# Fixing TensorE's order through the sample step of a two-layer streaming encoder, with gate products in thirds between its steps

## The chip, the cores and the metric

The kernel runs on one core of one Trainium2 chip. The metric is the time of one execution on the device, in microseconds (us), from the first to the last instruction with what lies around them. Three timed runs of the kernel before gave 2090.80, 2094.46 and 2092.82 us; their median is 2092.82 us. The profile was taken in an execution of its own.

The engines are called as in the profile: PE (TensorE, matrix products), DVE (VectorE), ACT (ScalarE), POOL (GpSimd) and SP (SyncE, which here only issues transfers). Each engine works through its own list of instructions in one order, and waits on semaphores for the others.

## What is computed

The reference is one step of an encoder with two layers, over a prompt of 2048 tokens and 8 samples of 16 tokens, 1024 wide, all in float32. Layer 0 is a diagonal complex state-space mixer (S5), layer 1 a gated delta rule mixer with 8 value heads and states of 128 x 128. Each layer normalizes, shifts, scales and gates with values made from a condition vector.

```python
for i in range(DEPTH):
    mod = silu(c) @ w_ada[i] + b_ada[i]
    shift, scale, gate = split(mod, 3)
    h = rms_norm(x, norm_g[i]) * (1 + scale) + shift
    out, state = s5_branch(h, ...) if i == 0 else gdn_branch(h, ...)
    x = x + gate * out
y = rms_norm(x, final_g)
```

The change lies in layer 1. Its branch projects h to queries, keys, values and a gate z, runs a short convolution over q, k and v, and then, chunk by chunk of 128 tokens and for each head, does the delta rule in matrix form: a triangular matrix made from keys, decays and betas is inverted; new values are that inverse times (beta v minus decayed keys times the old state); the output is decayed queries times the old state plus a masked product of queries and keys with the new values; the state is decayed and gets keys times new values. The output is normalized per head, multiplied by silu(z) and projected by `w_out`. The outputs are y, the states after prompt and samples, and the last rows before the convolution.

## The kernel before

Tokens are ordered in 17 tiles of 128: tiles 0 to 15 are the prompt, and tile 16 holds the 8 samples, each with a state of its own that comes from outside. All products of weights with activations are made in three parts (`mm3`, L148): high by high, high by low, low by high, where a number is split into a high part in a narrower format and the rest.

Layer 1 has these stages, in the order of the code:

- Blocks 0 to 15 (`conv_block`): q, k and v of all tokens, with convolution, written to DRAM as `kq_d` and `v_d`. Between them small triangular blocks are solved on DVE (`lane_solve`).
- Blocks 16 to 23: the gate z, in five column ranges `NATT` (widths 512, 512, 384, 384, 384). `gate_cols` (L1793) makes one block and range: 24 products into one PSUM tile, a SiLU on ACT, and a store to `zz_d` from ACT's queue (`store_heads`). Blocks 16 to 20 come first. Blocks 21 to 23 do their two wide ranges before the sample step; the nine narrow ones stay in the list `rest`, and `between` (L1935) makes one of them each time it is called.
- The entry to the sample step, L1903 to L1907: `load_x(0, 16)` loads tile 16 (keys and queries `kq`, row terms `ra` and `rb`, blocks of the inverse `xf`), adds masks on POOL and takes 16 or 8 exponentials on ACT (`decays`); `k_prod` makes keys by keys and queries by keys; `k_turn` and `v_turn` transpose keys and values on PE and scale them on DVE (`kup`, `bv`).
- The sample step (`sample`, L1390), a loop over 8 heads. `first(h)` loads the 8 samples' states of one head (`s0`, 512 KB) and multiplies keys and queries with them (L1407). `second(h)` takes the new values (L1418), copies them on ACT (`svn`, L1420), makes the output part (L1421), spreads the new values over the samples on DVE (`vm`, L1425), multiplies keys with them (L1428), adds into the states on DVE (L1431) and stores these from POOL's queue (L1433). After head 3 chunk 0 is loaded and its `k_prod` made, after head 5 its block inverse is finished (`invert`).
- The prompt loop (L2135), 16 chunks in order. Each carries the state `Sf` forward, in high and low parts `Sh` and `Sl`. The projection of one tile (`project`) is a generator whose pieces are put between the steps of later chunks, by the string of letters at L2184 (p for a piece of the projection, i for one of the next chunk's inverse, v for half of the next chunk's value turn). The sample tile's projection is the first of them; it leaves the products with the low part of the weight to the end (`late_low`, L2078).
- Before the loop, the last weight `w_out` is loaded (`w2_raw`, 8 parts of 512 KB) and split into high parts on ACT (L2114) and low parts on POOL (L2117).

The order of the work on each engine is set by a planner, which runs the program in a model of its own time and picks the earliest work in program order that is ready there. Two things bind it. `tc.issue_after(i)` (in `later`, L142) lets an instruction come only after `i` in the plan. And an `Engine` whose `ordered` is true puts each of its instructions behind the one before, so its list is just the order of the Python program. In the kernel before SP is ordered from L2121, DVE from L2131, and ACT, PE, DVE and POOL from L2140, at chunk 0; DVE and POOL go back to the planner at L2152, SP at L2182. In the sample step nothing is ordered.

The names that the steps below touch: `ssq` (sums of squares per head), `rs` (their reciprocal roots, made by `rsqrt`, L1347, with two ACT functions and small DVE operations on 8 columns), `oo` (outputs of a tile), `poT` (their transposes), `ob`, `ohi`, `olo` (gated, and split in high and low), `epo` (the projection), `psu` (keys by new values), `pvn` and `vn` (new values of a chunk), `epk` and `epv` (transposed keys and values), `fB` and `gB` (rows spread over all partitions), `ezt` (z of a tile). PSUM pools: `pso` with 2 buffers, `psh` with 4, `pse` with 2. The gate's activations of layer 1 (`h1h`, `h1l`) lie in the same memory as later the weight parts and the chunk's tiles.

## Time and profile before

| | kernel before |
|---|---|
| timed runs, median (3) | 2092.82 us |
| the profiled execution | 2091.16 us |
| its span, first to last instruction | 2089.4 us |
| PE busy | 2039.9 us (98%) |
| DVE busy | 1481.2 us (71%) |
| ACT busy | 1007.9 us (48%) |
| POOL busy | 507.5 us (24%) |
| mean granted PE clock | 0.991 |
| DMA | 343.74 MB, mean 165 GB/s |

In a row of a timeline stand start and length in us, engine, line, operation, what it writes and reads, and the count of like instructions merged; in brackets, the idle time of the engine before it and what ended that. L70 is the line of the helper that issues the instructions of ordered engines, so there the names tell more than the line. Rows with SPq or ACTq are issues of transfers. Matmul ends are modelled, so a group's length reaches a little over the start of the next.

### The profile page before, as it was taken

What the parts mean: (1) busy time and instruction counts of PE and PEld (TensorE: products, weight loads), DVE (VectorE), ACT (ScalarE), POOL (GpSimd) and SP (SyncE); (2) the same over time, 40 slices, a digit from 0 to 9 for tenths busy, and PEclk for the clock granted to TensorE, in tenths of its full rate; (3) what the DMA queues carried; (4) which work ended last, traced back from release to release, by engine and by line L of the source; (5) the groups of instructions that cost most, each with busy time, mean ns of one, the idle gap of its engine ahead of it and who ended that gap; (6) DMA issues with size and microseconds to landing.
All of it is one profiled execution on the core that took longest, in us unless ns stands there. A gap on an engine that the chain in (4) does not pass through costs nothing.

```text
span 2089.4 us, 41295 instructions
## 1 busy us (share of the span) xinstructions
PE 2039.9 (98%) x15473; PEld 1824.0 (87%) x15473; DVE 1481.2 (71%) x3401; ACT 1007.9 (48%) x2426; POOL 507.5 (24%) x759
## 2 busy tenths in 40 slices
PE   7999999999999999999999999999999699999998
PEld 5889988888999999999788879899987588888887
DVE  7988668777674455557555669687546888888885
ACT  4534445555454444446655322341224466666663
POOL 1268500000122222221100010110022444444430
PEclk8999999999999999999999999999999999999999
DMA  8798856666563333325665212753455734455532
GB/s 308 275 309 277 272 169 199 192 193 185 166 206 124 103 121 108 130 93 213 185 192 162 76 50 77 183 137 100 138 170 192 228 124 136 149 151 151 151 116 71
DMA packets 314611, 343.74 MB, mean 165 GB/s; under 512 B 88522, under 2 KB 261082, under 8 KB 311596
## 3 DMA queue, kind: packets, MB, share of 16 engines
q1 hardware_dynamic: 183196, 229.90, 35.6%
q10 hardware_dynamic: 125792, 94.38, 13.9%
q0 software_dynamic: 5424, 16.83, 2.2%
q8 instruction: 122, 2.00, 0.4%
q14 instruction: 77, 0.63, 0.1%
HBM read 220.81 MB, written 120.21 MB: 163 GB/s over the span
## 4 chain that ended last, share of the span: by engine, by line
PE 87%; DVE 5%; DMA 4%; ACT 3%; issue 1%; ACTq 0%; SPq 0%; POOL 0%; DVEq 0%
PE epo L70 8%; PE pdz L70 8%; PE pc L151 5%; PE pc L152 5%; PE pc L153 5%; PE po L153 3%; PE po L152 3%; PE pz L153 3%; PE po L151 3%; PE pz L151 3%; PE pz L152 3%; PE py L70 3%; PE pd L151 2%; PE pg L153 2%; PE pg L151 2%; PE pg L152 2%
## 5 line engine op out<-in xcount | busy, mean ns | idle before, releaser
L151 PE MATMUL pc<-h1h,wdh 128*128 128x512 f32 (+1 forms) x600 | 216.7, 361 | 0.8 <-ACT pb L1570 0.8
L152 PE MATMUL pc<-h1l,wdh 128*128 128x384 f32 (+1 forms) x600 | 215.1, 358 | 0.3 <-POOL h1l L1521 0.3
L153 PE MATMUL pc<-h1h,wdl 128*128 128x384 f32 (+1 forms) x600 | 215.1, 359 | 0.0
L1581 DVE SCALAR_TENSOR_TENSOR ac<-pb,convw,ac 128x384 f32<-128x384 f32 (+3 forms) x288 | 163.7, 592 | 3.3
L151 PE MATMUL po<-gh,woh 128*128 128x272 f32 x512 | 147.9, 292 | 1.7 <-ACT woh L137 1.1
L153 PE MATMUL po<-gh,wol 128*128 128x272 f32 x512 | 148.9, 292 | 0.4 <-DVE wol L139 0.4
L152 PE MATMUL po<-gl,woh 128*128 128x272 f32 x512 | 148.3, 291 | 0.1
L70 PE MATMUL pdz<-hhz,wzh 128*128 128x272 f32 x448 | 131.1, 293 | 0.4 <-ACT evz L70 0.4
L152 PE MATMUL pg<-yl,wgh 128*128 128x272 f32 x448 | 130.0, 290 | 0.0
L151 PE MATMUL pg<-yh,wgh 128*128 128x272 f32 x448 | 129.4, 289 | 0.0
L70 PE MATMUL pdz<-hhz,wzl 128*128 128x272 f32 x448 | 129.3, 289 | 0.0
L153 PE MATMUL pg<-yh,wgl 128*128 128x272 f32 x448 | 129.2, 288 | 0.0
L70 PE MATMUL pdz<-hlz,wzh 128*128 128x272 f32 x448 | 128.8, 288 | 0.0
L151 PEld LDWEIGHTS pc<-h1h,wdh 128*128 128x128 f32 x600 | 112.8, 188 | 13.0 <-ACT pb L1570 1.7
L152 PEld LDWEIGHTS pc<-h1l,wdh 128*128 128x128 f32 x600 | 112.8, 188 | 10.5 <-issue 0.8
L153 PEld LDWEIGHTS pc<-h1h,wdl 128*128 128x128 f32 x600 | 112.7, 188 | 10.1 <-issue 0.8
L151 PE MATMUL pd<-hh,wuh 128*128 128x272 f32 x384 | 112.4, 295 | 2.8 <-ACT hh L229 2.8
L70 PE MATMUL epo<-w2h,ohi 128*128 128x512 f32 x272 | 111.7, 411 | 0.0
L153 PE MATMUL pd<-hh,wul 128*128 128x272 f32 x384 | 111.1, 290 | 0.0
L152 PE MATMUL pd<-hl,wuh 128*128 128x272 f32 x384 | 111.1, 290 | 0.0
L1104 POOL TENSOR_TENSOR zt<-zt,sz 128x272 f32<-128x272 f32 x64 | 61.7, 970 | 192.1 <-ACT sz L1103 188.9
L70 PE MATMUL epo<-w2h,olo 128*128 128x512 f32 x272 | 107.1, 394 | 0.0
(651 smaller groups left out, 6329.4 us busy)
## 6 DMA issues: line engine op xcount, KB each, us to landing
wa<-in_w_ada SPq DMA_DIRECT2D x32, 512.0 KB
wdr<-in_w_in SPq DMA_DIRECT2D x24, 512.0 KB
u_d<-ev ACTq DMA_DIRECT2D x64, 136.0 KB
...
```

Source lines behind the costliest of these rows:

```text
L70: i_ = f(*a, **kw)
L151: T.matmul(ps, lhsT=w_hi[k], rhs=x_hi[k], start=(k == 0), stop=False)
L152: T.matmul(ps, lhsT=w_hi[k], rhs=x_lo[k], start=False, stop=False)
L153: i_ = T.matmul(ps, lhsT=w_lo[k], rhs=x_hi[k], start=False, stop=(k == n - 1))
L1104: G.tensor_mul(zt, zt, sz)
L1581: V.scalar_tensor_tensor(o, src(j), convw[:, b, j:j + 1], o, op0=ALU.mult, op1=ALU.add)
```

## The change

It does these things.

- `sample` calls `between` three times for a head: after `svn` has been copied, after `vm` has been made, and at the end of the head.
- `gate_cols` is divided: `gate_products` makes the 24 products in parts and stops after each, and `gate_store` does the SiLU and the store. The nine narrow blocks become a generator `fills` that gives 27 thirds (9, 9 and 6 products); each call of `between` takes one.
- PE is ordered from the wide gate blocks of 21 to 23 to the end of the sample step.
- In the entry, `k_turn` of tile 16 comes after two thirds, `v_turn` after a third one.
- Chunk 0 is loaded after head 2 (in the plan behind the activation of the last stored block), its `k_prod` comes after head 4, and its inverse runs in one piece per call from head 5 on. The gate blocks are no longer held behind chunk 0's exponentials.
- The low part of `w_out` is made in four quarters of 256 columns. Only parts 0 to 2 are split before chunk 0; high parts 3 to 7 come inside chunk 0 behind the new values, their low parts behind the new state.
- In chunk 0 the sample tile's gate comes first, then the new values, the products of the new state (`state_products`, taken out of `new_state`) and the transposes of chunk 1's keys (`k_transposes`, taken out of `k_turn`), then the transposes of the sample tile (`split`) and the first piece of its projection, and only then the rest of the new state.
- The letters of chunk 0 become "v v p p i p i p" in place of "p p p i v v p i p".

```diff
--- before.py
+++ after.py
@@ -1259,13 +1259,17 @@
         else:
             mm3(ps, [p["kh"][:, s, :]], [p["kl"][:, s, :]], [rh], [r])
 
-    def k_turn(p, E=G):
+    def k_transposes(p):
+        pk = pse.tile([P, 4, P], F32, tag="e", name=f"epk{p['t']}")
+        for h in range(4):
+            T.transpose(pk[:, h, :], p["kq"][:, h, :], ident)
+        return pk
+
+    def k_turn(p, E=G, pk=None):
 
         n, t, kq, kh = (p[i] for i in ("n", "t", "kq", "kh"))
         p["kup"] = kup = epar(n).tile([P, 8, P], F32, tag="kup", name=f"kup{t}")
-        pk = pse.tile([P, 4, P], F32, tag="e", name=f"epk{t}")
-        for h in range(4):
-            T.transpose(pk[:, h, :], kq[:, h, :], ident)
+        pk = pk or k_transposes(p)
         V.tensor_mul(kup.rearrange("p (h r) i -> p h r i", r=2), bc(pk, 2, 2),
                      bc(sc["ku"][:, t].rearrange("p (h r) -> p h r", r=2), 3, P))
         if kh is not None:
@@ -1418,11 +1422,13 @@
             T.matmul(p2[:, 0], lhsT=x[:, h, :], rhs=r, start=True, stop=True)
             vn = es.tile([P, P], F32, tag="sr", name=f"svn{h}")
             S.copy(vn, p2[:, 0])
+            between(h, 0)
             T.matmul(p2[:, 1], lhsT=pt_[:, h, :], rhs=vn, start=True, stop=True)
             V.tensor_add(oo[:, h], oo[:, h], p2[:, 1])
             S.activation(p2[:, 1], oo[:, h], AF.Square, accum_out=ssq[:, h:h + 1])
             vm = (eb1 if h % 2 else ea1).tile([P, 8, P], F32, tag="S", name=f"vm{h}")
             V.tensor_mul(vm, bc(vn, 1, 8), bc(seq, 2, P))
+            between(h, 1)
             for hf in range(2):
                 p4 = psh.tile([P, 4, P], F32, tag="h", name=f"sp4{h}_{hf}")
                 T.matmul(p4, lhsT=kup[:, h], rhs=h4(vm, hf), start=True, stop=True)
@@ -1437,7 +1443,7 @@
             nxa = first(h + 1) if h < 7 else None
             second(h, *a)
             a = nxa
-            between(h)
+            between(h, 2)
         return lambda zt: gate(t, oo, ssq, zt)
 
 
@@ -1790,9 +1796,17 @@
                 nc.sync.dma_start(row_d[w_, 0:128, :], ro[:, 0])
                 nc.sync.dma_start(row_d[w_, 128:136, :], ro[0:8, 1])
 
+        def gate_products(b, w, n0, n, pool, tag, parts=(None,)):
+            ps = pool.tile([P, 512], F32, tag=tag, name=f"pz{b}_{n0}")[:, 0:n]
+            for part in parts:
+                mm3(ps, [w[0][:, k] for k in range(KC)], [w[1][:, k] for k in range(KC)], *hcols(n0, n), part)
+                yield ps
+
         def gate_cols(b, w, n0, n, pool, tag):
-            ps = pool.tile([P, 512], F32, tag=tag, name=f"pz{b}_{n0}")[:, 0:n]
-            mm3(ps, [w[0][:, k] for k in range(KC)], [w[1][:, k] for k in range(KC)], *hcols(n0, n))
+            ps, = gate_products(b, w, n0, n, pool, tag)
+            return gate_store(b, n0, n, ps)
+
+        def gate_store(b, n0, n, ps):
             ac = d3.tile([P, 512], F32, tag="ac", name=f"az{b}_{n0}")[:, 0:n]
             silu = S.activation(ac.rearrange("p (c s) -> p c s", s=8), by_token(ps, n), AF.Silu).ins
             store_heads(zz_d, b - 16, n0, n, ac)
@@ -1902,14 +1916,13 @@
             nc.sync.dma_start(g1_d[:, 512 * hf:512 * hf + 512], g9[0:9])
         p16 = load_x(0, 16)
         k_prod(p16)
-        k_turn(p16)
         load_v(p16)
-        list(v_turn(p16))
 
         wz = {21: wnext}
         t_ = pbp.tile([P, 2, KC, P], F32R, tag="pb", name="wd23")
         wz[22] = load_blk(22 * P, dst=(t_[:, 0], t_[:, 1]))
         wz[23] = load_blk(23 * P)
+        T.ordered, T.last = True, None
         for b, w in wz.items():
             for n0, n in NATT[0:2]:
                 gate_cols(b, w, n0, n, pso, "o")
@@ -1928,25 +1941,41 @@
         y64 = {1: eb1.tile([P, 8, 64], F32, name="y641")}
         for z_ in (xf[1], y64[1]):
             G.memset(z_, 0.0)
-        rest = [(b, w, n0, n) for n0, n in NATT[2:] for b, w in wz.items()]
-
-        p0 = {}
-
-        def between(h=8):
-
-            with later([p0["ex"]] if p0 else []):
-                i_ = gate_cols(*rest.pop(0), pso, "o")
-            if h == 3:
-                with later([i_]):
+        p0, silus, inv = {}, [], []
+
+        def fills():
+            for n0, n in NATT[2:]:
+                for b, w in wz.items():
+                    for ps in gate_products(b, w, n0, n, pso, "o", (range(3), range(3, 6), range(6, KC))):
+                        yield
+                    silus.append(gate_store(b, n0, n, ps))
+
+        fill = fills()
+
+        def between(h, step):
+
+            next(fill, 0)
+            if step == 2 and h == 2:
+                with later(silus[-1:]):
                     p0.update(load_x(1, 0))
-                    k_prod(p0)
-            if h == 5:
-                list(invert(p0))
-            return i_
-
+            if step == 2 and h == 4:
+                k_prod(p0)
+            if step == 2 and h == 5:
+                inv.append(invert(p0))
+            for i in inv:
+                next(i, 0)
+
+        for _ in range(2):
+            next(fill)
+        k_turn(p16)
+        next(fill)
+        list(v_turn(p16))
         sample_gate = sample(p16, between)
-        while rest:
-            last_silu = between()
+        for _ in fill:
+            pass
+        list(inv[0])
+        last_silu = silus[-1]
+        T.ordered = False
     if upto == "D":
         return dict(kq_d=kq_d, v_d=v_d, zz_d=zz_d, row_d=row_d, x1n_d=x1n_d, nd_d=nd_d, xd_d=xd_d, yd_d=yd_d)
 
@@ -2008,14 +2037,20 @@
                 S.copy(vn, p2)
                 p["vn"].append(vn)
 
-        def new_state(p):
-            t, kup = p["t"], p["kup"]
+        def state_products(p):
+            ps = []
+            for hf in range(2):
+                ps.append(psh.tile([P, 4, P], F32, tag="h", name=f"psu{p['t']}_{hf}"))
+                for i in range(4):
+                    T.matmul(ps[hf][:, i], lhsT=p["kup"][:, 4 * hf + i, :], rhs=p["vn"][hf][:, i], start=True, stop=True)
+            return ps
+
+        def new_state(p, ps):
+            t = p["t"]
             nh = ea1.tile([P, 8, P], F32R, tag="S", name=f"Sh{t}")
             nl = eb1.tile([P, 8, P], F32R, tag="S", name=f"Sl{t}")
             for hf in range(2):
-                p3 = psh.tile([P, 4, P], F32, tag="h", name=f"psu{t}_{hf}")
-                for i in range(4):
-                    T.matmul(p3[:, i], lhsT=kup[:, 4 * hf + i, :], rhs=p["vn"][hf][:, i], start=True, stop=True)
+                p3 = ps[hf]
                 if t == 0:
                     V.tensor_copy(h4(Sf, hf), p3)
                 else:
@@ -2110,11 +2145,15 @@
             for k in ks:
                 SY.dma_start(w2_raw[k], I["w_out1"][k * P:(k + 1) * P])
 
-        def split_w2(k):
+        def high_w2(k):
             S.copy(w2_hi[k], w2_raw[k])
+
+        def low_w2(k):
             if k:
                 w2_lo[k] = e1.tile([P, D], F32R, tag=f"w2r{k - 1}", name=f"w2l{k}")
-            nc.gpsimd.tensor_sub(w2_lo[k], w2_raw[k], w2_hi[k].bitcast(F32))
+            for q in range(4):
+                c = slice(256 * q, 256 * q + 256)
+                G.tensor_sub(w2_lo[k][:, c], w2_raw[k][:, c], w2_hi[k][:, c].bitcast(F32))
 
         y64[0] = eb.tile([P, 8, 64], F32, name="y640")
         G.memset(y64[0], 0.0)
@@ -2125,8 +2164,9 @@
         zt = load_z(16)
         gates = project_rows(16)
         pp = {0: p0, 1: load_x(2, 1, True)}
-        for k in range(KC):
-            split_w2(k)
+        for k in range(3):
+            high_w2(k)
+            low_w2(k)
         k_turn(p0)
         V.ordered = True
         list(v_turn(p0))
@@ -2139,13 +2179,18 @@
                 for e in (S, T, V, G):
                     e.ordered = True
                 Sf = e1.tile([P, 8, P], F32, tag="Sf", name="Sf")
+                split = sample_gate(zt)
                 new_values(p)
-                split = sample_gate(zt)
+                ps_, pk_ = state_products(p), k_transposes(nx)
+                for k in range(3, KC):
+                    high_w2(k)
+                prev = project(16, *split(), gates)
+                next(prev)
+                new_state(p, ps_)
+                for k in range(3, KC):
+                    low_w2(k)
                 keys_high(nx)
-                prev = project(16, *split(), gates)
-                new_state(p)
-                next(prev)
-                k_turn(nx, V)
+                k_turn(nx, V, pk_)
                 masks(nx, V)
                 decays(nx)
                 out = outputs(p)
@@ -2171,7 +2216,7 @@
                     decays(nx)
             next(prev)
             if t > 0:
-                new_state(p)
+                new_state(p, state_products(p))
                 out = outputs(p)
             split = gate(*out)
             if nx:
@@ -2181,7 +2226,7 @@
                 masks(pp[t + 2])
             SY.ordered = False
             iv, vv = (invert(nx), v_turn(nx)) if nx else (none, none)
-            for s in ("p i p p i p v v" if 0 < t < 15 else "p p p i v v p i p" if t == 0 else "p p p").split():
+            for s in ("p i p p i p v v" if 0 < t < 15 else "v v p p i p i p" if t == 0 else "p p p").split():
                 next({"p": prev, "i": iv, "v": vv}[s], 0)
             if t < 14:
                 keys_high(pp[t + 2])
```

## The prediction

> **What bounds the kernel now.** First the page: its second part shows TensorE (PE) at 9 tenths in nearly every slice.
>
> ```profile
> PE   7999999999999999999999999999999699999998
> ```
>
> One slice inside the run stands at 6; with 52.2 us to a slice it covers 1619 to 1671 us, the end of the sample step and the first chunk of the prompt loop. Then the view by windows: us of the stretch, busy us of PE, PE's weight load, DVE, ACT, POOL (with counts), granted PE clock, DMA share, GB/s.
>
> ```profile
> 1453.00:1463.00 10.00, 10.00 (x60) 10.00 (x59) 7.49 (x24) 2.62 (x3) 0.56 (x1) 1.00 0.23 70
> 1559.00:1611.64 52.64, 52.64 (x405) 39.98 (x403) 31.88 (x88) 19.63 (x54) 6.84 (x7) 1.00 0.45 140
> 1611.64:1618.00 6.36, 4.50 (x25) 1.98 (x24) 4.92 (x14) 3.67 (x8) 5.89 (x4) 0.73 1.04 407
> 1618.00:1626.50 8.50, 6.06 (x52) 3.79 (x53) 7.18 (x10) 4.85 (x9) 8.32 (x4) 1.00 1.04 363
> 1626.50:1638.00 11.50, 1.85 (x18) 1.69 (x17) 10.22 (x15) 3.47 (x6) 8.19 (x5) 0.68 1.02 260
> 1638.00:1642.00 4.00, 4.00 (x24) 4.00 (x25) 3.14 (x6) 1.24 (x2) 0.00 (x0) 0.63 0.32 90
> 1642.00:1673.00 31.00, 27.02 (x264) 22.98 (x263) 24.85 (x49) 17.74 (x58) 10.79 (x6) 1.00 0.67 205
> ```
>
> Up to 1611.64 PE never idles, because gate products fill every gap; the sample step's last two heads then run without filling. Only this idle time can be won. The three rows from 1611.64 to 1638.00 hold 1.86 + 2.44 + 9.65 = 13.95 us of it, and 1642 to 1673 holds 3.98. PE's own timeline names the waits, in brackets:
>
> ```profile
> 1612.90 3.08 PE L1428 MATMUL sp<-vm,kup 128*128 128x512 f32 x4 [1.26 <-DVE vm L1425]
> ...
> 1619.57 0.66 PE L1268 MATMUL epk<-ident,ekq 128*128 128x128 f32 x4
> 1620.50 0.49 PE L1418 MATMUL sp<-sr,xf 128*128 128x128 f32 x2 [0.28 <-DVE sr L1411]
> ...
> 1621.67 1.06 PE L1298 MATMUL epv<-ident,evt 128*128 128x128 f32 x8
> 1624.54 1.99 PE L1428 MATMUL sp<-vm,kup 128*128 128x512 f32 x4 [1.81 <-DVE vm L1425]
> 1626.36 1.95 PE L70 MATMUL pvn<-bv,xf 128*128 128x128 f32 x16
> 1637.95 1.94 PE L70 MATMUL poT<-ident,oo 128*128 128x128 f32 x8 [9.65 <-DVE oo L70]
> 1639.69 2.56 PE L70 MATMUL psu<-vn,kup 128*128 128x128 f32 x16
> ```
>
> After a gap the same products run slower: L1428 takes 3.08 against 1.99 us, and 16 psu take 2.56 against 1.95 for 16 pvn of that shape, where the clock row reads 0.73 or 0.63. The slow clock costs 1.09 + 0.61, and about 0.97 on poT (8 in 1.94, half of pvn's 1.95 would do); I put 1.1 on the small products of the inverse in the 0.73 row. That is 3.8 us, so 1611.64 to 1642.00 lies 17.7 us above its work at full speed, 12.7 us.
>
> The 9.65 us is the vector engine's chain to `oo`, and the next two views (DVE, then POOL) show why it is long:
>
> ```profile
> 1629.94 2.47 DVE L70 TENSOR_TENSOR ntth<-rs 128x8 f32<-128x8 f32 x1 [1.15 <-ACT rs L70]
> 1632.44 0.17 DVE L70 TENSOR_TENSOR ntth<-ntth,nmsh 128x8 f32<-128x8 f32 x1
> 1632.64 2.21 DVE L70 TENSOR_SCALAR ntth<-ntth 128x8 f32<-128x8 f32 x1
> ...
> 1635.09 3.32 DVE L70 TENSOR_TENSOR oo<-oo,rs 128x512 f32<-128x512 f32 x2
> 1639.08 1.60 DVE L70 SCALAR_TENSOR_TENSOR ob<-poT,ngd,ezt 128x512 f32<-128x512 f32 x2 [0.67 <-PE poT L70]
> 1640.60 1.46 DVE L70 TENSOR_TENSOR olo<-ob,ohi 128x512 fp32r<-128x512 f32 x2
> ```
>
> ```profile
> 1618.59 8.12 POOL L2117 TENSOR_TENSOR w2l<-w2r,w2h 128x1024 fp32r<-128x1024 f32 x3
> ...
> 1630.02 7.24 POOL L2117 TENSOR_TENSOR w2l<-w2r,w2h 128x1024 fp32r<-128x1024 f32 x3
> 1643.39 2.54 POOL L70 TENSOR_TENSOR Sl<-Sf,Sh 128x512 fp32r<-128x512 f32 x2 [6.13 <-ACT Sh L70]
> ```
>
> Operations on 8 columns take 2.47 and 2.21 us exactly while POOL works through `w2l`, and 0.17 between: they wait for one POOL instruction each.
>
> **The change part by part.** The sum is made against the profiled execution, 2091.16 us (span 2089.4). The three timed runs have a median of 2092.82, 1.66 above it; I add that at the end.
>
> *Entry.* Both turns of tile 16 (`epk`, `epv`) go behind 3 thirds of gate products. Work is the same, and products that wait for nothing surround them: 0. If that cover failed, the price would be their own 0.66 + 1.06 us.
>
> *Sample step, filled.* 24 products take 24 x 10.00/60 = 4.0 us, so thirds of 9, 9 and 6 last 1.5, 1.5 and 1.0 us. The 27 thirds are just the 3 of the entry and 24 between the steps of 8 heads. Each hides a short chain (here two of its links, from groups by line, 1559 to 1612, with mean ns, and what stands before them on ACT):
>
> ```profile
> L1425 DVE TENSOR_TENSOR vm<-svn,seq 128x1024 f32<-128x1024 f32 x7 | 8.6, 1222 | 1.3 <-ACT svn L1420 1.3
> ...
> L1420 ACT COPY svn<-sp 128x128 f32<-128x128 f32 x7 | 1.8, 263 | 8.8 <-PE sp L1418 8.8
> ...
> L1250 ACT ACTIVATE erb<-erb,sc_cb 128x128 f32<-128x128 f32 x8 | 3.1, 389 | 0.0
> L1252 ACT ACTIVATE era<-era,sc_cb 128x128 f32<-128x128 f32 x8 | 3.1, 387 | 0.0
> L1250 ACT ACT_TABLE_LOAD x1 | 1.3, 1283 | 0.0
> ```
>
> `svn` (0.26) fits in a third, and `vm` (1.22) has two thirds. What is new is that PE can no longer go round a late step. Chunk 0's 16 exponentials and their table load stand before an `svn` on ACT: 6.2 + 1.3 us of busy time against a cover of 1.5. Chunk 0's ten loads on SP, now placed behind the third block, have two heads until `k_prod`, about 15 us (7 `vm` lie in 52.64 us): 5.5 to land, two masks of 2.4 on POOL (both rows below), and that ACT block make 17.8, so they may be 3 late and hold the same `svn`. The gate activations are no longer held behind the exponentials, so more table loads at 1.28 are possible. Between 0 and 5 us lost; I take 2.0, because the block meets one head of eight, and only what is left of it counts.
>
> *The end of the sample step.* Let time run from the end of the last third. Gate products now last until then, and so does the store of z that tile 16's `ezt` needs. On the SP queue, in written order, `ezt` stands before two more loads and chunk 1's keys `ekq`; `k_transposes(nx)` needs these, and it now stands before poT in TensorE's order. In ACT's and SP's timelines:
>
> ```profile
> 1608.87 0.49 ACT L1797 ACTIVATE az<-pz 128x384 f32<-128x384 f32 x1
> 1609.39 0.39 ACTq L1537 DMA_DIRECT2D zz_d<-az  x1
> ...
> 1625.08 1.03 ACT L2114 CAST w2h<-w2r 128x1024 fp32r<-128x1024 f32 x1
> ...
> 1634.21 1.04 ACT L70 CAST ekh<-ekq 128x1024 fp32r<-128x1024 f32 x1 [4.30 <-DMA ekq<-kq_d]
> 1639.86 0.62 ACT L70 CAST ohi<-ob 128x512 fp32r<-128x512 f32 x1 [4.61 <-DVE ob L70]
> ```
>
> ```profile
> 1619.35 0.33 SPq L70 DMA_DIRECT2D ezt<-zz_d  x1
> ...
> 1649.32 0.38 SPq L70 DMA_DIRECT2D erb<-row_d  x1
> ```
>
> ```profile
> 1654.85 2.41 POOL L1245 TENSOR_TENSOR erb<-erb,maskB 128x1024 f32<-128x1024 f32 x1 [8.91 <-DMA erb<-row_d]
> ```
>
> ```profile
> DMA to landing us min/median/max: 3.5/6.1/8.4
> ```
>
> The activation and the store's issue end at about 1.1. The store took 9.6 us (1609.78 to 1619.35) beside a DMA share of 1.04; the state's stores (last row) took 3.5 at best, and with the weights loaded earlier I take 3.5: `ezt` leaves at 4.6. From there the keys took 14.9 us (1619.35 to 1634.21), in the same crowd. The second load of a later group took 5.5 (1649.32 to 1654.85); two more of 512 KB at 363 GB/s add 1.4 each. I take 8.5: keys at 13.1, with bounds 4.6 + 5.5 = 10.1 and 4.6 + 14.9 = 19.5. Work to hand before them: the turns of tile 0 1.72, pvn 1.95, psu 1.95, together 5.6. So 7.5 us idle; the rest of the 9.65 is not won, its releaser only changes from DVE to DMA. The vector chain itself, without POOL, would be there earlier; five high parts of 1.03 on ACT, between `vn` and `ohi`, also end inside that wait (price without it: up to 5.2). Behind the keys epk and poT run at the slow clock (1.6 more), then `ob` 0.75, `ohi` 0.62 and `olo` 0.73 lie open (2.1), since psu, which covered them, has gone ahead; 0.5 for a slow start of epo. Together 11.7 in place of 17.7: a gain of 6.0 (9.0 with early keys, a loss of 0.4 with late ones).
>
> The Trainium skill, in TensorE: Matmul & The Clock Gate, Part 1, halves the clock after an idle window of about 3.4 us and restores it after one as long of work. By that the new wait costs 1.7 instead of my 2.1, and the sum would be 0.4 better; but the 0.73 row follows a gap of only 1.26, which that rule would let pass, so the trace agrees only in part.
>
> *Low parts in quarters.* `Sl`, 512 wide, takes 1.27 a piece and `w2l`, 1024 wide, 2.41 to 2.71; on that line a quarter costs about 0.7 (estimate; 0.6 if nothing is fixed, 1.3 if it costs as much as `Sl`). Eight parts add some 3 us to POOL. Parts 3 to 7 now stand behind `Sl` on POOL, which ended 3.9 us after epo began (1645.93 against 1642.00): 20 quarters end at about 18. The first low product stood here:
>
> ```profile
> L70 PE MATMUL epo<-w2l,ohi x18: 387/390/398, 1653.1 to 1673.8; 128*128 128x512 f32 x18
> ```
>
> That is 11.1 after epo began; with both value turns ahead of it, waiting on DVE, it comes at 13 to 15, and its eighth needs the last part 1.6 later. A wait of 1 to 2 us: 1.5 lost (bounds: 1.5 won out of the 3.98 us idle there, and 6 lost). SP waits too: `fB` lies in the last raw part's memory, and z of chunk 0 and the keys and rows of chunk 2 queue behind it, over 10 us later than now; their use is a chunk away: 0.5, at most 3.
>
> Sum: 6.0 - 2.0 - 1.5 - 0.5 = 2.0 us won: 2089.2 for a profiled execution, 2090.8 beside the timed runs.
>
> **The rivals.** *The filling pays in full*: keys at 10.1 (3.0 more), no lost step (2.0), parts in time (1.5): 8.5 won, 2084.3. For it: PE without idle to 1611.64 in much the same mixture, and a DMA share of 0.45 there. Against it: `ezt` cannot leave before the last gate store lands.
>
> *The late low parts decide*, slower: POOL works on them beside DVE's masks, and a quarter pays its fixed part four times. If a quarter took 1.03 us, 20 of them would end 6.6 later, PE's first low products would wait for it, and `fB` would hold SP as long: 2097.4. The point is thus near 1.0 us a quarter; above it slower, below it no. For it: POOL took 8.12 for three beside DVE against 7.24. Against: the line through both widths says 0.7.
>
> *The order written is nearly the one that the planner had*, and thirds change nothing: 2092.8. Against: heads 6 and 7 ran bare.
>
> **How the numbers follow.** From no change this kernel's timing can tell 0.2%, 4.2 us. The forecast has 0.42, the full filling 0.35, late low parts 0.19, an unchanged order 0.04. Of the forecast's share 0.03 lies beyond 4.2 us on the fast side and 0.01 on the slow one. So faster 0.38, within 0.2% 0.42, slower 0.20. The range, 2084.3 to 2097.4, ends at the two rivals; its unknowns are the keys' landing, the ACT block, and a quarter's price.
>
> **What would show it.** Right: the windows of the sample step without idle to the last third; the longest PE wait in front of epk, released by the DMA of `ekq`, 6 to 9 us; the 8-column operations at 0.2 to 0.9 us; a PE wait of 1 to 2 us on `w2l`. Wrong: a PE wait on `svn` or `sr` in many heads (step two), poT still waiting for `oo`, keys there before psu ends, or the low products waiting over 6 us.

## The result, and the profile after

The changed kernel takes 2110.64 us (median of 4 runs, 2108.27 to 2113.76), the kernel before 2091.81 us in the runs beside them (2085.97 to 2094.46). The ratio is 1.0098, with a 95% interval of 1.0083 to 1.0113: 19 us slower, where 2.0 faster was forecast, and beyond the slow end of the range, 2097.4. The profiled execution took 2112.45 us, with a span of 2110.7. Of the kernels tried below, one execution of the last took 2599.32 us at a mean granted clock of 0.72, its ten others 2086.48 to 2092.23; the slow one is left out of that kernel's time and ratio.

The page's second part again shows a slice at 6 tenths at the same place, between 1636 and 1688 us of the longer span, and now also one at 8, between 1530 and 1583, inside the sample step:

```profile
PE   7999999999999999999999999999989699999998
```

Five marks cut the stretch around it, the same in both kernels: the products pg (behind block 20, 1510.97 before and 1511.07 after); the end of the sample step's last product, `sp` or `pz`; the first product epo of tile 16; the end of pvn of chunk 1; the start of pvn of chunk 2. They give four stages: the sample step with its entry (S1), its end (S2), the loop of chunk 0 (S3), chunk 1 (S4). The view by windows, with the columns of the prediction, of the kernel before and then of the changed one:

```profile
1510.97:1626.53 115.56, 111.25 (x715) 87.82 (x714) 68.76 (x175) 42.35 (x92) 30.18 (x24) 0.99 0.59 188
1626.53:1642.00 15.47, 5.82 (x40) 5.66 (x40) 13.33 (x20) 4.71 (x8) 8.16 (x5) 0.67 0.83 216
1642.00:1673.06 31.06, 27.08 (x264) 23.04 (x263) 24.85 (x49) 17.74 (x58) 10.79 (x6) 1.00 0.67 204
1673.06:1698.04 24.98, 24.98 (x257) 21.86 (x257) 18.91 (x42) 16.08 (x53) 12.84 (x8) 1.00 0.33 99
```

```profile
1511.07:1627.86 116.79, 109.98 (x707) 87.06 (x706) 67.81 (x179) 37.28 (x88) 17.68 (x19) 0.97 0.54 174
1627.86:1648.61 20.75, 9.07 (x53) 7.88 (x51) 6.53 (x14) 11.93 (x14) 10.07 (x13) 0.67 0.77 212
1648.61:1689.55 40.94, 32.74 (x257) 27.29 (x258) 30.82 (x50) 19.30 (x60) 27.49 (x26) 0.83 0.39 126
1689.55:1719.00 29.45, 26.80 (x257) 23.16 (x256) 18.88 (x44) 16.06 (x53) 12.71 (x8) 0.94 0.43 134
```

The differences are +1.2, +5.3, +9.9 and +4.5, together 20.9 of the 21.3 us by which the spans differ; behind chunk 2's pvn next to nothing is lost. Three things stand out. S1 did not become shorter though its idle time was to be filled: PE idles 116.79 - 109.98 = 6.8 us in it (before: 4.3). And POOL, with 10.79 us of work in S3 before, has 27.49. And of the 9.9 us in S3 only 4.2 are idle time of PE (8.2 against 4.0): the other 5.7 are its products, nearly the same ones, which took 32.74 us in place of 27.08 at a granted clock of 0.83 in place of 1.00.

PE's waits in the changed kernel, from 1550 to 1720, in us in total, times and longest (the longest, without one on `qt`):

```profile
PE epk L70 <- DMA ekq<-kq_d: 7.9, 1, 7.9
PE sp L70 <- ACT svn L1424: 4.8, 2, 3.3
PE epg L70 <- POOL ekl L1277: 2.6, 1, 2.6
PE epv L70 <- issue: 2.3, 1, 2.3
PE psu L70 <- ACT vn L70: 2.0, 1, 2.0
...
PE epo L70 <- POOL w2l L70: 1.6, 1, 1.6
```

The wait on the keys is there as forecast. What stands on ACT ahead of `svn`, from ACT's timeline (start, us):

```profile
1571.63 0.49 ACT L1811 ACTIVATE az<-pz 128x384 f32<-128x384 f32 x1 [3.55 <-PE pz L70]
1572.14 1.28 ACT L1250 ACT_TABLE_LOAD   x1
...
1577.24 0.39 ACT L1252 ACTIVATE era<-era,sc_cb 128x128 f32<-128x128 f32 x1
1577.53 0.24 ACT L1424 COPY svn<-sp 128x128 f32<-128x128 f32 x1
```

A table load and 14 of the 16 exponentials run before the copy, which PE's next product needs: 3.25 us of waiting. POOL's timeline and two stretches of SP's:

```profile
1631.71 9.34 POOL L2156 TENSOR_TENSOR w2l<-w2r,w2h 128x256 fp32r<-128x256 f32 x12 [2.40 <-ACT w2h L2149]
1651.47 2.54 POOL L70 TENSOR_TENSOR Sl<-Sf,Sh 128x512 fp32r<-128x512 f32 x2 [10.42 <-ACT Sh L70]
1653.95 18.18 POOL L70 TENSOR_TENSOR w2l<-w2r,w2h 128x256 fp32r<-128x256 f32 x20
```

```profile
1632.49 0.33 SPq L70 DMA_DIRECT2D ezt<-zz_d  x1
...
1634.12 0.85 SPq L70 DMA_DIRECT2D ekq<-kq_d  x1
...
1672.16 0.33 SPq L70 DMA_DIRECT2D fB<-in_fg  x1
...
1673.06 0.39 SPq L70 DMA_DIRECT2D ekq<-kq_d  x1
```

A quarter takes 0.78 us in the first group and 0.91 in the second. Before the second, POOL stands idle for 10.42 us, in order behind `Sl`, which waits for the state and so for poT and the keys. `fB` leaves 0.03 us after the last low part, and chunk 2's keys behind it, 24 us later than before (1648.90).

### The profile page after: what moved, and what is told of

Same layout as the page of the kernel before. It is cut to its first block, busy times and chain, and to the rows that moved or that the text cites. A ratio compares the mean times of both kernels' runs of the same rounds, so it can differ in the third digit from the quotient of the medians.

```text
span 2110.7 us, 41313 instructions
## 1 busy us (share of the span) xinstructions
PE 2050.6 (97%) x15473; PEld 1831.3 (87%) x15473; DVE 1477.0 (70%) x3401; ACT 1011.7 (48%) x2429; POOL 512.3 (24%) x783
## 4 chain that ended last, share of the span: by engine, by line
PE 86%; DMA 5%; ACT 4%; DVE 4%; issue 1%; POOL 0%; SPq 0%; ACTq 0%; DVEq 0%
PE pdz L70 8%; PE epo L70 8%; PE pc L151 5%; PE pc L152 5%; PE pc L153 5%; PE py L70 3%; PE pz L70 3%; PE po L153 3%; PE po L152 3%; PE po L151 3%; PE pd L151 2%; PE pg L153 2%; PE pg L151 2%; PE pg L152 2%; PE pd L152 2%; PE pd L153 2%
## 5 line engine op out<-in xcount | busy, mean ns | idle before, releaser
L151 PEld LDWEIGHTS pc<-h1h,wdh 128*128 128x128 f32 x600 | 112.6, 188 | 12.9 <-issue 1.7
L70 PE MATMUL epo<-w2l,ohi 128*128 128x512 f32 x272 | 106.9, 402 | 1.8 <-POOL w2l L70 1.6
```

The costliest lines, as they stand in the source:

```text
L70: i_ = f(*a, **kw)
L151: T.matmul(ps, lhsT=w_hi[k], rhs=x_hi[k], start=(k == 0), stop=False)
```

## The experiments

The stages S1 to S4 of every kernel, each from one execution, by the same five marks (the windows of some are shown); times are medians, ratios go against the kernel before on the same chip. In kernels with the same S1 it differs by up to 3.4 us between executions, so smaller differences in it say nothing. In the paced kernels, below, 20 small products (1.3 us) lie in S2 instead of S1. The column behind S3 has PE's idle time in it and its mean granted clock. The rest of S3 is PE's work, 257 to 264 matmuls in every kernel: it took 27.1 us in the kernel before and up to 34.1 at the lowest clock, so a longer S3 is not all waiting.

| kernel | S1 | S2 | S3 | idle, clock in S3 | S4 | sum | time | ratio (95%) |
|---|---|---|---|---|---|---|---|---|
| before | 115.6 | 15.5 | 31.1 | 4.0, 1.00 | 25.0 | 187.1 | 2091.8 | |
| changed | 116.8 | 20.8 | 40.9 | 8.2, 0.83 | 29.5 | 207.9 | 2110.6 | 1.0098 (1.0083-1.0113) |
| sample step alone | 115.1 | 25.1 | 32.1 | 2.4, 0.88 | 25.0 | 197.2 | 2101.5 | 1.0050 (1.0033-1.0067) |
| chunk 0 alone | 113.7 | 14.4 | 38.3 | 7.2, 0.90 | 26.1 | 192.4 | 2094.9 | 1.0026 (1.0016-1.0035) |
| fB later | 115.5 | 21.5 | 43.2 | 10.5, 0.83 | 25.0 | 205.2 | 2110.7 | 1.0101 (1.0086-1.0116) |
| whole parts | 115.5 | 19.9 | 36.9 | 7.7, 0.86 | 25.0 | 197.3 | 2100.5 | 1.0053 (1.0038-1.0068) |
| low parts early | 115.9 | 21.8 | 35.6 | 5.9, 0.89 | 26.3 | 199.7 | 2102.5 | 1.0061 (1.0043-1.0080) |
| keys first | 113.4 | 17.6 | 38.0 | 6.5, 0.89 | 26.4 | 195.4 | 2103.0 | 1.0062 (1.0047-1.0076) |
| quarters alone | 113.7 | 13.0 | 32.9 | 3.1, 0.88 | 25.0 | 184.5 | 2088.7 | 0.9995 (0.9986-1.0004) |
| chunk 0, whole | 113.1 | 14.4 | 36.9 | 8.3, 0.91 | 25.0 | 189.4 | 2094.8 | 1.0026 (1.0015-1.0037) |
| sample paced | 106.3 | 22.9 | 38.3 | 6.6, 0.88 | 32.1 | 199.6 | 2105.8 | 1.0078 (1.0057-1.0099) |
| psu first | 113.7 | 7.9 | 40.9 | 8.1, 0.81 | 25.0 | 187.5 | 2092.6 | 1.0010 (1.0000-1.0020) |
| paced, keys, low early | 106.3 | 12.9 | 37.2 | 7.9, 0.91 | 26.8 | 183.1 | 2084.7 | 0.9977 (0.9967-0.9987) |
| paced, old chunk 0 | 106.9 | 20.4 | 36.7 | 3.4, 0.79 | 25.0 | 188.9 | 2093.7 | 1.0016 (1.0004-1.0028) |
| ... mixed parts | 106.3 | 13.0 | 41.5 | 10.5, 0.84 | 26.4 | 187.1 | 2093.7 | 1.0015 (1.0005-1.0024) |
| ... rows earlier | 106.7 | 12.8 | 37.3 | 4.1, 0.78 | 25.0 | 181.8 | 2085.6 | 0.9981 (0.9972-0.9989) |
| ... both of these | 106.9 | 13.3 | 41.4 | 10.6, 0.84 | 26.3 | 187.8 | 2091.5 | 1.0010 (1.0001-1.0019) |
| ... old letters | 107.9 | 12.8 | 42.9 | 8.8, 0.76 | 25.0 | 188.6 | 2090.5 | 1.0001 (0.9992-1.0010) |
| ... letters, DVE | 106.3 | 12.6 | 39.9 | 9.2, 0.87 | 25.0 | 183.8 | 2088.6 | 0.9993 (0.9984-1.0002) |

**Which half.** The change was taken apart: entry and sample step alone (`state_products`, `high_w2` and `low_w2`, the order at `t == 0` and the letters put back), and the rest alone (`between`, `fills` and the entry put back).

The first, at its core (the second has the same lines the other way round):

```diff
-                split = sample_gate(zt)
                 new_values(p)
-                ps_, pk_ = state_products(p), k_transposes(nx)
-                for k in range(3, KC):
-                    high_w2(k)
+                split = sample_gate(zt)
+                keys_high(nx)
                 prev = project(16, *split(), gates)
+                new_state(p)
                 next(prev)
-                new_state(p, ps_)
-                for k in range(3, KC):
-                    low_w2(k)
-                keys_high(nx)
-                k_turn(nx, V, pk_)
+                k_turn(nx, V)
```

> The changed kernel with chunk 0's order, the planning of the low parts (whole, ahead of chunk 0) and the letters put back as before; the entry and the sample step in thirds stay. Theory A (three stages lose, one after the other: sample step, its end, chunk 0 with what queues behind its loads): the sample step still loses the 7 to 9 us that the trace shows between 1552 and the last third, and most of the rest of the 19 is gone: 2097 to 2102 us. Theory B (only the late low parts and the loads behind them cost; the sample step's waits are absorbed by the wait for oo that stood there before): 2089 to 2093 us. If the sample step alone carries the whole loss: 2108 to 2112.

> The changed kernel with entry and sample step as before (whole gate products, order left to the planner, exponentials not held back from them); chunk 0's order, the quarters and the letters of the change stay. Theory A: chunk 0 and its queue still lose, the sample step does not: 2099 to 2106 us. Theory B (the late low parts and the loads behind them are all of it): 2107 to 2113 us. If the loss came from the sample step alone: 2089 to 2094.

The first was measured at 2101.5, the second at 2094.9. Each half loses by itself, 10 and 5 us by their ratios; the whole change loses 20 by its ratio, 5 more than the sum, which is within the intervals of the three. The sample step alone gains nothing in S1 and loses 9.6 us in S2: PE waits 13.98 us for `oo`. Two things make that wait. DVE stands 7.96 us until ACT has made `rs`, which there comes behind the casts of all eight high parts; after that DVE's operations run beside low parts, which are whole there (2.20 us for one on 8 columns):

```profile
1638.20 1.67 DVE L70 TENSOR_TENSOR ntth<-rs 128x8 f32<-128x8 f32 x1 [7.96 <-ACT rs L70]
```

Chunk 0 alone gains in S2 and loses 7.2 us in S3. Theory A's range holds for the first run; the second came in 4 us below A's range, and 1 us above that in which the sample step carries the whole loss. Theory B, that only what follows the late low parts costs, is out in both.

**The load queue.** The issue of `fB` was moved.

```diff
-                SY.dma_start(fB, dram_ap(I["fg"], 0, [[0, P], [1, D]]))
 ...
                 pp[t + 2] = load_x(t + 3, t + 2, True)
+                if t == 0:
+                    SY.dma_start(fB, dram_ap(I["fg"], 0, [[0, P], [1, D]]))
```

> The changed kernel with one issue moved: the load of fB, which in the changed kernel waits on SP until 1672.16 for the last low part, is issued behind the loads of chunk 2 (z of chunk 0, keys, rows, x, y), so that these no longer stand behind it. Theory A: what chunk 1 loses (PE's 1.95 on qt, the slow pvn, 2.65 on ekl, 4.5 us of delay after chunk 0) goes: 2102 to 2106 us. Rival (these loads would be late for memory or for the low parts themselves, so the queue is only where it shows): 2109 to 2112.

2110.7 us: no change, so theory A missed here. S4 shows the gain, 29.5 to 25.0, and S3 and the wait for the keys give it back. With chunk 2's rows there earlier, POOL takes their masks ahead of the low parts:

```profile
1661.80 2.36 POOL L1245 TENSOR_TENSOR erb<-erb,maskB 128x1024 f32<-128x1024 f32 x1
...
1666.88 2.33 POOL L1244 TENSOR_TENSOR era<-era,maskA 128x1024 f32<-128x1024 f32 x1
1669.18 6.39 POOL L70 TENSOR_TENSOR w2l<-w2r,w2h 128x256 fp32r<-128x256 f32 x8
```

The last part ends at 1675.57 instead of 1672.13, and PE waits 8.0 us for `w2l` in place of 1.6. So it is POOL's work, and not the queue alone, that is late.

**The pieces.** Low parts whole again.

```diff
-            for q in range(4):
-                c = slice(256 * q, 256 * q + 256)
-                G.tensor_sub(w2_lo[k][:, c], w2_raw[k][:, c], w2_hi[k][:, c].bitcast(F32))
+            G.tensor_sub(w2_lo[k], w2_raw[k], w2_hi[k].bitcast(F32))
```

> The changed kernel with each low part made by one instruction of 1024 columns, in place of four of 256; order and places unchanged. If the fixed part of four pieces is what makes them late (20 took 18.2 us from 1653.95 to 1672.13; five whole ones at 2.4 to 2.7 take 12 to 13.5), fB leaves 5 us sooner and the 1.57 us wait on w2l goes: 2103 to 2107 us. If the pieces are not slower in sum beside DVE (POOL waits for DVE either way) or whole ones hold DVE's small operations as long as they did before: 2109 to 2114.

2100.5 us, 10 less than the changed kernel and better than expected. The five late parts take 14.86 us in place of 18.18:

```profile
1651.36 14.86 POOL L70 TENSOR_TENSOR w2l<-w2r,w2h 128x1024 fp32r<-128x1024 f32 x5
```

S3 is 4.1 and S4 4.5 us shorter. The same edit in the order of chunk 0 alone, and the pieces by themselves in the kernel before:

> The order of chunk 0 alone, as in the run that kept the old sample step (2094.9 us), but with whole low parts. There epo began at 1637.28 against 1642.00 before, and the loop then lost 7.2 us. From the whole parts in the changed kernel (10 us) I expect at least half here, since the sample step is shorter and the parts start sooner: 2086 to 2090 us. If the order itself (both value turns first, parts behind Sl) carries what was lost: 2093 to 2096 us.

> The kernel before with its eight low parts made in quarters, nothing else. DVE's operations on 8 columns took 2.47 and 2.21 us there because each waited for one whole low part on POOL. If pieces of 0.7 to 0.9 us let DVE in sooner, oo is ready 2 to 4 us earlier and PE's 9.65 shrinks to 6 to 8: 2086 to 2089 us. If the parts as a whole end later by their fixed cost (eight parts, 3 to 5 us on POOL) and the chunk then waits for them: 2090 to 2094 us.

2094.8 against 2094.9: there the pieces cost no time that shows, and the rival of that expectation holds. In the kernel before, quarters make 2088.7 us, a ratio whose interval holds 1. Its PE waits 5.9 us for `oo` in place of 9.65, as hoped, and S3 gives 1.8 us back, at a clock of 0.88 and with less idle time. The pieces take POOL longer (18.18 against 14.86), and that hurts only where POOL's work stands on the path.

**POOL's order and the keys.** One move each: the quarters of parts 3 to 7 ahead of `new_state`, and `load_x(2, 1, True)` ahead of `load_z(16)` and `project_rows(16)`.

```diff
                 for k in range(3, KC):
                     high_w2(k)
+                for k in range(3, KC):
+                    low_w2(k)
                 prev = project(16, *split(), gates)
                 next(prev)
                 new_state(p, ps_)
-                for k in range(3, KC):
-                    low_w2(k)
```

```diff
+        pp = {0: p0, 1: load_x(2, 1, True)}
         zt = load_z(16)
         gates = project_rows(16)
-        pp = {0: p0, 1: load_x(2, 1, True)}
```

> The changed kernel with one move in POOL's order: the quarters of parts 3 to 7 stand ahead of Sl, right behind the high parts they need, instead of behind it. In the changed kernel POOL idles 10.42 us in front of Sl (1641.05 to 1651.47) and then works 18 us on the quarters; the run with fB moved showed that the load queue alone is not the cause (2110.7). Theory C (POOL's order: its work of the chunk begins 10 us too late, everything behind it follows): the parts end near 1658, fB leaves then, PE's 1.57 on w2l, 1.95 on qt and 2.65 on ekl go: 2099 to 2104 us. Rival (it is the price of the pieces, 18 us against 15 for whole ones, wherever they stand): 2107 to 2112.

> The changed kernel with the loads of chunk 1 (keys, rows, x, y) issued on SP ahead of z of tile 16 (which waits for the last gate store), so that PE's 7.92 us in front of epk, released by the DMA of the keys, falls away and poT waits for oo alone (ready at 1633.39). If the wait for the keys is on the path: epo starts 6 to 8 us sooner and the time is 2102 to 2106 us. Rival (the low parts on POOL decide what comes after, so an early epo only waits longer for them): 2108 to 2112 us.

2102.5 and 2103.0 us: each takes off some 8 us, so both waits were on the path. With the parts early S3 falls by 5.3 us, though the wait for the keys is 10.1 there. With the keys first the wait of 7.92 us on epk becomes one of 7.41 on `ohi`: z of tile 16, now at the end of the queue, is what is late next (`ezt` leaves at 1639.94, and DVE's `ob`, which reads it, starts at 1643.58). S2 falls by 3.2, S3 by 3.0, S4 by 3.0.

**The sample step.** ACT's order is written out, and the exponentials are halved.

```diff
-            if step == 2 and h == 2:
-                with later(silus[-1:]):
-                    p0.update(load_x(1, 0))
-            if step == 2 and h == 4:
+            if step == 2 and h == 2:
+                p0.update(load_x(1, 0, True))
+                masks(p0)
+            if step == 1 and h in (4, 5):
+                decays(p0, range(4 * h - 16, 4 * h - 12))
+            if step == 2 and h == 5:
                 k_prod(p0)
-            if step == 2 and h == 5:
+            if step == 2 and h == 6:
                 inv.append(invert(p0))
 ...
+        S.ordered = SY.ordered = True
         sample_gate = sample(p16, between)
```

> The changed kernel with the sample step's ACT and SP work placed by hand: ACT and SP in written order, chunk 0's ten loads behind the fourth state load, its 16 exponentials in two halves of 8 behind the Squares of heads 4 and 5, k_prod and the inverse one head later. From the row of pg (about 1511) to the end of the sample step's last product the changed kernel took 116.8 us, the kernel before 115.6 and, with quarters only, 113.7: the filled step gained nothing. Theory D (the waits on svn, 1.56 and 3.25, with the slow clock behind them, ate the filling: ACT's block and the early loads are the cause): the stretch falls to 109.5 to 112.5 us, and the time by 3 to 6 us to 2104 to 2108. Rival (the step has other links that a third does not cover: vm, the buffers of sp, and the clock): the stretch stays above 114 and the time within 2 us of 2110.6.

S1 falls to 106.3 us, more than expected (1.3 of the 10.5 are the small products that went to S2), and PE idles 0.85 us in it:

```profile
1511.67:1617.94 106.27, 105.42 (x687) 83.96 (x687) 65.61 (x178) 35.29 (x84) 18.43 (x19) 1.00 0.59 183
```

Theory D holds for its part on ACT. SP's order was in fact the same before the edit, and the loads of chunk 0 leave at 1547.66 to 1557.11, against 1546.17 to 1555.40 in the changed kernel, so they were not the cause. What changed at head 0 is that the copy stands ahead of the SiLU and the store of z; at heads 4 and 5 the exponentials come after the head's short steps. In the changed kernel the store was issued 5.1 us after its SiLU, and the copy stood behind it (for what the store waited the profile does not say); first the changed, then the paced kernel:

```profile
1551.12 0.49 ACT L1811 ACTIVATE az<-pz 128x384 f32<-128x384 f32 x1 [0.26 <-PE pz L70]
1556.71 0.37 ACTq L1543 DMA_DIRECT2D zz_d<-az  x1
...
1557.46 0.26 ACT L1424 COPY svn<-sp 128x128 f32<-128x128 f32 x1
```

```profile
1556.24 0.26 ACT L70 COPY svn<-sp 128x128 f32<-128x128 f32 x1
...
1557.81 0.49 ACT L70 ACTIVATE az<-pz 128x384 f32<-128x384 f32 x1
1558.40 0.37 ACTq L1543 DMA_DIRECT2D zz_d<-az  x1
```

Yet the time is only 5 us below the changed kernel's. PE waits 10.8 us for the keys, whose loads did not move up with it.

**Psu first, in the kernel before.** With quarters, of the new order at `t == 0` only three moves: `sample_gate` ahead of `new_values`, `state_products` ahead of poT, `keys_high(nx)` behind the first products.

```diff
-                new_values(p)
                 split = sample_gate(zt)
-                keys_high(nx)
+                new_values(p)
+                ps_ = state_products(p)
                 prev = project(16, *split(), gates)
-                new_state(p)
+                new_state(p, ps_)
                 next(prev)
+                keys_high(nx)
```

> The kernel before with quarters for the low parts, and of the reordering of chunk 0 only this: the gate of tile 16 (its Ln, Exp) is placed ahead of the new values on ACT, the products psu ahead of poT on PE, the copy of the next keys behind ohi and the first products. Low parts, keys' transposes and letters stay where the kernel before has them. With quarters alone PE waited 5.89 us in front of poT, psu then took 3.6 at the slow clock behind it, and ohi waited for the copy of the keys (1638.10 to 1639.15). If the change's idea is right and only its late parts were wrong: epo begins 2 to 4 us earlier after the sample step than with quarters alone (12.97 us), and the time is 2085 to 2088. If ob and olo lie open for what psu covered: 2088 to 2091.

2092.6: neither. S2 falls from 13.0 to 7.9, more than hoped, and S3 gives it all back, 40.9 against 32.9. Chunk 1 comes sooner, and now DVE's two products for `oo` of chunk 0 fall beside the two masks on POOL:

```profile
1657.67 4.98 DVE L1374 TENSOR_TENSOR oo<-oo,rs 128x512 f32<-128x512 f32 x2
```

```profile
1657.00 2.35 POOL L1245 TENSOR_TENSOR erb<-erb,maskB 128x1024 f32<-128x1024 f32 x1 [8.98 <-DMA erb<-row_d]
1659.30 2.80 POOL L1244 TENSOR_TENSOR era<-era,maskA 128x1024 f32<-128x1024 f32 x1
```

PE waits 3.8 us for them at poT, and S3's mean clock is 0.81: 5.1 of the 8.1 us are idle time, 3.0 slower products.

**All three places.** The paced step with the low parts early and only the keys, not all loads of chunk 1, issued ahead of raw parts 5 to 7:

```diff
         load_w2(0, 1, 2, 3, 4)
         load_v(p0)
+        kq1 = load_k(2, 1)
         load_w2(5, 6, 7)
 ...
-        pp = {0: p0, 1: load_x(2, 1, True)}
+        pp = {0: p0, 1: load_x(2, 1, True, kq1)}
```

> The paced sample step (106.3 us from pg to its last product, 2105.8 us in all) with two further edits to the change: the quarters of parts 3 to 7 ahead of Sl on POOL, and the keys of chunk 1 issued right behind chunk 0's values, ahead of raw parts 5 to 7 and of z of tile 16. There PE waited 10.78 us in front of epk for these keys and, in the low products, 0.55 and 2.36 on w2l. If the three places add (sample step, keys, POOL's order): the wait on the keys goes, what is left is a wait of 3 to 6 us on ohi for z of tile 16, epo begins 14 to 18 us behind the sample step in place of 22.9, and the time is 2090 to 2096. Rival (the transfers as a whole are the limit there, about 400 GB/s from the weights' loads on: what is put ahead delays the rest as much): epo begins 20 us or more behind it, and the time stays at 2100 to 2105.

> The paced sample step of the change with chunk 0 as the kernel before has it (low parts, in quarters, planned ahead of it; keys behind the first products; old letters), the gate of tile 16 alone put ahead of the new values. The sample step then ends some 9 us sooner than before (106.3 against 115.6), and z of tile 16 lands some 12 us later than its last product in place of long before it. If the step's gain is kept behind it: epo begins 15 to 17 us behind it (before: 15.5), the loop takes 32 to 33 as before, and the time is 2082 to 2087. If the weights and chunk 1's loads set the pace (they leave SP only when the sample step's tiles are free): the loop waits for low parts or keys, and the time is 2088 to 2093.

2084.7 us, below the expected range: faster than both kernels, 26 below the changed one and, by the ratio, 0.23% below the one before. The wait on the keys is gone, and S2 is 12.9 us (S2 and S3):

```profile
1615.82:1628.69 12.87, 8.25 (x74) 6.68 (x73) 9.32 (x16) 11.71 (x17) 9.74 (x13) 1.00 0.78 261
1628.69:1665.87 37.18, 29.30 (x257) 24.74 (x258) 28.42 (x49) 19.27 (x60) 27.97 (x28) 0.91 0.73 216
```

With the old chunk 0 behind the paced step it is 2093.7, above both expected ranges: S2 stays at 20.4, since PE waits 6.35 us on `ohi`, and S3 is 36.7, with 3.4 us of idle time and products at 0.79. But that wait is again one for the keys, which the old order copies on ACT ahead of `ohi`:

```profile
1637.69 1.05 ACT L70 CAST ekh<-ekq 128x1024 fp32r<-128x1024 f32 x1 [7.14 <-DMA ekq<-kq_d]
1638.64 1.13 ACT L70 CAST ohi<-ob 128x512 fp32r<-128x512 f32 x2
```

This kernel has the loads of the changed one, and the old order with early keys was not run. If just those 6.35 us went, it would take some 2087 (an estimate). So what the change's order of chunk 0 is worth by itself stays open.

**What is left in S3.** Five kernels on the one of 2084.7 us (the lines with dots in the table): parts 3 to 7 whole; rows, x and y of chunk 1 ahead of the gate rows; both; the old letters; the old letters with parts 6 and 7 made by DVE.

```diff
-            for q in range(4):
-                c = slice(256 * q, 256 * q + 256)
+            n = 4 if k < 3 else 1
+            for q in range(n):
+                c = slice(D // n * q, D // n * (q + 1))
```

```diff
-        gates = project_rows(16)
         pp = {0: p0, 1: load_x(2, 1, True, kq1)}
+        gates = project_rows(16)
```

> The kernel with paced sample step, early keys and the low parts ahead of Sl (2084.7 us), and parts 3 to 7 made by one instruction each, 0 to 2 still in quarters while DVE's short operations run. There the loop from the first epo to the end of pvn of chunk 1 takes 37.2 us against 31.1 before, and PE waits 4.56 in front of epv while POOL works on quarters to 1647.13, about 0.83 each. If the price of the pieces sets the loop: five parts at 2.4 to 3.0 in place of 3.3 end 3 to 4 us sooner and the time is 2081 to 2083. If the rows of chunk 1 set it (masks at 1637.67, exponentials to 1645.65): 2084 to 2086.

> The same kernel (2084.7 us), with the rows, x and y of chunk 1 issued on SP ahead of the gate rows and x1 of tile 16, which are first read behind the low products. DVE waits 2.41 us there for era to land (1637.67), and the masks, 16 exponentials and epv follow. If the rows set the loop: the masks start 2 to 3 us sooner and the time is 2081 to 2083. If the low parts do, which end at 1647.13 whatever the rows do: 2084 to 2086.

> Both of the two edits before. If each of the two chains ends at the same time, as the trace suggests (exponentials and epv 1647.11, low parts 1647.13), neither edit alone is worth much and both together 2 to 4 us: 2080 to 2083. If one alone set the loop, this equals the better of the two runs before.

Whole parts end 2.9 us sooner here too (1644.21 against 1647.13), and yet the kernel is 8 us slower by the ratios, where 2 to 4 faster or no change was expected. DVE's timeline says why, first of the kernel with quarters, then of that with whole parts:

```profile
1628.67 2.01 DVE L70 TENSOR_TENSOR olo<-ob,ohi 128x512 fp32r<-128x512 f32 x2
...
1631.80 1.21 DVE L70 TENSOR_TENSOR kup<-epk,sc_ku 128x1024 f32<-128x1024 f32 x1
1633.51 1.75 DVE L70 TENSOR_TENSOR ekl<-ekq,ekh 128x1024 fp32r<-128x1024 f32 x1 [0.51 <-ACT ekh L70]
1637.67 1.47 DVE L70 TENSOR_TENSOR era<-era,maskA 128x1024 f32<-128x1024 f32 x1 [2.41 <-DMA era<-row_d]
1639.07 1.75 DVE L70 TENSOR_TENSOR erb<-erb,maskB 128x1024 f32<-128x1024 f32 x1
```

```profile
1629.41 3.48 DVE L70 TENSOR_TENSOR olo<-ob,ohi 128x512 fp32r<-128x512 f32 x2
...
1634.01 1.21 DVE L70 TENSOR_TENSOR kup<-epk,sc_ku 128x1024 f32<-128x1024 f32 x1
1635.72 2.96 DVE L70 TENSOR_TENSOR ekl<-ekq,ekh 128x1024 fp32r<-128x1024 f32 x1 [0.51 <-ACT ekh L70]
1639.36 2.65 DVE L70 TENSOR_TENSOR era<-era,maskA 128x1024 f32<-128x1024 f32 x1 [0.68 <-DMA era<-row_d]
1641.93 3.36 DVE L70 TENSOR_TENSOR erb<-erb,maskB 128x1024 f32<-128x1024 f32 x1
```

Beside whole parts each operation that reads two tiles waits for one long POOL instruction, and `olo` with the masks takes 4.3 us longer, 5.5 with `ekl`; the exponentials and the value turns behind them are late, and PE waits 6.95 us there in place of 4.56. S3 accounts for 4.3 us of that; the profiled execution, at 2090.2, was one of the fastest of its 12 (2089.0 to 2097.6), and where the slower ones lose more is not shown. Rows earlier change nothing (2085.6), although S4 is 1.8 us shorter in its trace. But they did what they were meant to do: the masks start 6.5 us after the first epo in place of 9.0, and PE's waits in front of the two value turns fall from 4.56 and 1.34 us to 0.77 and 0.76. PE's products took that back: 33.24 us in place of 29.30. S3 with earlier rows, and with the old letters, which come next:

```profile
1630.74:1668.06 37.32, 33.24 (x257) 28.30 (x258) 30.32 (x49) 19.18 (x60) 27.70 (x27) 0.78 0.71 203
1629.23:1672.13 42.90, 34.06 (x257) 28.93 (x258) 31.45 (x50) 19.43 (x60) 31.57 (x29) 0.76 0.69 200
```

So DVE's chain from the rows to the value turns did hold PE, and shortening it gained nothing because the clock was lower in that execution; whether it was in the other ten is not shown. With whole parts POOL's long instructions hold the same chain, and earlier rows do not clearly help (2091.5).

```diff
-            for s in ("p i p p i p v v" if 0 < t < 15 else "v v p p i p i p" if t == 0 else "p p p").split():
+            for s in ("p i p p i p v v" if 0 < t < 15 else "p p p i v v p i p" if t == 0 else "p p p").split():
```

```diff
-                for k in range(3, KC):
+                for k in range(3, 6):
                     low_w2(k)
 ...
                 out = outputs(p)
+                for k in (6, 7):
+                    low_w2(k, V, 1)
```

> The kernel with paced sample step, early keys and low parts ahead of Sl (2084.7 us), with the letters of chunk 0 as before the change: three steps of products first (both halves of the low products, one residual), value turns later. There PE stood 4.56 and 1.34 us in front of the value turns, which wait for buffers that the masks and exponentials of chunk 1 hold until 1647, and the low products came behind them from 1647.85. If the letters cost that: PE does low products while the exponentials run, as far as the low parts are there, and the time is 2080 to 2083. If the low parts, which end at 1647.13, hold the products as long as the buffers hold the turns: 2084 to 2087.

> The old letters again, and low parts 6 and 7 made by DVE in one instruction each behind its copy of oo, so that POOL has 12 quarters less (8 of these two parts, 0.83 each, are 6.6 us). If POOL's work on the low parts is what holds the loop: parts 0 to 5 end near 1640.5, DVE's two near 1645, the low products run from about 1641 and the time is 2078 to 2082, 2 us or more below the run with the letters alone. If DVE is then the one that is late (its masks, exponentials and products of era and erb stand beside it): no gain over the letters alone, or a loss.

The old letters cost 5 us by the ratios. PE waits 2.4 us for a low part, and then 4.4 in front of epq, a product of chunk 1's inverse, for which the profile names no releaser; the waits of 4.56 and 1.34 are gone. Its idle time in S3 thus grows by 1.0 us only, and the other 4.8 are its products at a clock of 0.76. The new letters are worth their place here, though by the trace more for the clock than for the waits. Work taken off POOL gives back at most 2 us (2088.6), which is not clear of noise. None of the five kernels is faster, against what was expected of each.

## Why the prediction was wrong

In the order of its steps:

- *Entry, 0.* Not tested by itself. `epk` and `epv` of tile 16 stand in a stretch without a gap over 0.2 us; nothing speaks against it.
- *Sample step, 2.0 lost, 0 to 5.* This step failed. The same 707 products took 107.32 us of PE at full clock in one of the experiments:

```profile
1514.04:1627.47 113.43, 107.32 (x707) 85.06 (x706) 67.62 (x179) 37.29 (x88) 17.68 (x19) 1.00 0.56 178
```

  Against that the changed kernel's S1 is 9.5 us long, 6.8 of idle time and 2.7 of slow clock, and the five others with the same step lose 6.1 to 8.6. The mechanism was named, ACT's block ahead of one `svn`, and it made one wait of 3.25 us. Missed were the wait at head 0 (1.56, behind a store of z on ACT's list), the one on `vm` beside POOL's masks (1.15), and the slow clock after them. With ACT's order written out the idle time is 0.85: shown by the paced kernel. Which of its parts, halves, order or the later `k_prod`, gives how much was not tried.
- *End of the sample step, 6.0 won.* The wait was right in place and size: 7.92 us in front of epk, released by the keys, against 7.5. `ezt` left 4.6 us after the last third, as said; the keys came at 17.3, not 13.1, within the bounds of 10.1 to 19.5. Not foreseen were 2.01 us of waiting on `vn` and 1.11 on `kup`, both behind ACT and DVE work that the planner had put first, and psu at 3.20 us in place of 1.95. So the keys came 4.2 us later and the work before them took 3.8 longer than forecast, and that the size of the wait fits is luck. Nor were all 6.0 us won: S1 and S2 together are 6.5 us longer, where 4.0 shorter was forecast. Of these 10.5 us 7.5 are the sample step's (9.5 lost in place of 2.0), and the other 3.0 belong here. The operations on 8 columns took 0.17 us, as said.
- *Chunk loop, 1.5 lost, between 1.5 won and 6 lost.* This step failed most: S3 is 9.9 us longer, outside the bounds. The quarter was sized at 0.7 and took 0.91, and the last part ended 23.5 us after epo began, not 18; PE's wait on `w2l`, forecast at 1 to 2, was 1.57. But the sum looked only at that wait. Of the 9.9 us, 4.2 are idle time of PE, 2.34 of it in one wait in front of the value turns, and 5.7 are products at a clock of 0.83, for which the sum had nothing. That POOL's late and long list, some 28 us of 41, brings this about is shown so far: parts early and parts whole each take 8 to 10 us off the time, 5.3 and 4.1 of it in S3. By which wait the list slows the clock stays open: with whole parts S3 has 7.7 us of idle time in place of 8.2, and its products are 3.6 us shorter.
- *SP queue, 0.5, at most 3.* S4 lost 4.5 us, and with `fB` out of the way it is 25.0 again, as it is with whole parts. The term was too small; as a remedy the move is worth nothing, since POOL then works on masks first.
- *The rival on the other side*, late low parts, had the right sign. Its point, 1.0 us a quarter, was not reached, and its price, 2097.4, took the sample step and the queue as they were forecast. The rival in which filling pays in full is what the paced step shows for S1, and no kernel with the change's own loads got to keep it.

Of the clock the prediction cited the Trainium skill, TensorE: Matmul & The Clock Gate, Part 1. The traces again agree only in part: see the last section.
